# First expert's input from products of tokens with scaled one-hots, gates and clearings taken out of the expert choice's chain, router loads issued from GpSimd

## The chip, the cores and the metric

The kernel runs on one core of a Trainium2 chip. The metric is the device time of one execution in microseconds (us); the number compared is the median of several executions. The chip's engines appear under the profile's names: PE is TensorE (PEld its weight loads), DVE is VectorE, ACT is ScalarE, POOL is GpSimd, SP is SyncE; a "q" behind the name is the engine's own queue of DMA issues and waits.

## What is computed

Two transformer layers over 512 tokens of width 1024. Each layer has a token mixer (the first one sliding-window attention and gated linear attention, the second one block attention), then a mixture of experts: 4 groups of 8 experts, a router that takes one group and the two best experts in it, and a gated hidden layer of 512. The part that matters here, cut from the reference:

```python
def _hier_moe(h, w_group, b_group, w_expert, b_expert, w1, w3, w2):
    g_logits = (xt @ w_group).astype(f32) + b_group.astype(f32)
    g_sel = jnp.argmax(g_logits, axis=-1)
    p_g = jnp.take_along_axis(jax.nn.softmax(g_logits, axis=-1), g_sel[:, None], axis=-1)
    ...
    top_v, top_i = lax.top_k(e_in, MOE_TOPK)
    gate = (p_g * jax.nn.softmax(top_v, axis=-1)).reshape(-1)
    ...
        xr = xt[tok]
        return (jax.nn.silu(xr @ w1[e]) * (xr @ w3[e])) @ w2[e]
# in the layer
h = _rms(x, norm2_w[layer]) * (1 + scale2) + shift2
x = x + gate2 * _hier_moe(h, ...)
```

## The kernel before, in words

The loop over the two layers holds an attention stage and an expert stage. The end of the attention stage makes, for each of four tiles of 128 tokens, the root mean square factor `r2` and the router's logits `lgt` (`norm2`, L587), and writes the scaled tokens to a table in DRAM, `h2d` (L590, from POOL's queue).

The choice (L1000 to L1088) runs mostly on DVE. Three full-size matmuls that nothing reads ("busy", L1002) are put on TensorE at its start. Then come the maxima and one-hots of group and experts, for three tiles together and for the last tile alone, ranks by small matmuls with triangular ones (L1059), and the table `rd` (L1066), which holds for each token and expert its place in that expert's window of 64 slots. Behind `rd`, in the same stretch, the gates are made (L1070 to L1088, with three ACT functions).

The expert stage is in an order written out by hand (`manual_schedule`): each engine takes its instructions as the program states them. It works with pairs of experts, 64 slots each. `select` (L1099) makes a pair's 0/1 matrix from tokens to slots. `gather` (L1132) sums token numbers through it on TensorE and fetches the 128 rows from `h2d` by an indirect DMA on POOL's queue into one of two buffers `xg`; slots without a token get a number out of bounds, and their rows are left as they were, which is why both buffers are cleared before the loop (L1357). `flip_rows` transposes the rows, and `modulate` scales and shifts them into `xT`. For the first pair this stands ahead of the loop: casts of `toknum`, two clearings, two selections and fetches, four more unread matmuls ("py", L1364), then `flip_rows_fast`. In the loop an expert has stage 1 (L1182: 16 products of `xT` with 4 weight tiles), SiLU and product on ACT and DVE, a transpose (L1189), stage 2 (L1202), and the way back into `x_t` (L1219, L1227). For the first expert both slot gates `gs` (L1128) of the first two pairs stand ahead of the product of L1405.

The weights come in 1 MB tiles, six for each expert, through the ring of slots `wA` (3), `wC` (2) and `wB` (13 for each layer, whose memory the attention stage uses before). All are issued on SP's queue (L178 and L181), in order, each when its slot is free: the first four slots of an expert when stage 1 has read them, the other two after stage 2. DMAs issued from SP and from ACT take turns on the same few completion semaphores; one whose turn falls on a semaphore waits until the DMA that had it before has landed. DMAs issued from POOL have others. `load_router` (L114 to L117) loads the router's weights `wr` and biases `br` for a layer, from ACT's queue: for the first layer at the start, for the second one as soon as the first layer's logits (for `br`) and the tables that lie on `wr` (for `wr`) have been used.

## Time and profile before

| | |
|---|---|
| median of 3 runs | 1637.0 us (1635.42 to 1642.87) |
| the profiled execution | 1640.46 us |
| its span, first to last instruction | 1638.7 us |
| mean granted TensorE clock | 0.963 |
| TensorE busy | 1477.0 us, 90% of the span |
| DVE, ACT, POOL busy | 917.0, 514.1, 338.1 us |
| read from HBM | 506.31 MB |

The rows further down are from this one execution; their times are us from the start of its span, its own time is 3.5 us over the median. A stretch's DMA share is the mean busy share of the 16 DMA engines, and PEclk the granted clock of TensorE, where 1.00 is 2.4 GHz and 0.50 is 1.2 GHz. The chain that ended last is followed back by the page only to the branch that closes the second layer's loop; it tells nothing of the stage that is changed, so that stage is read from timelines and stretches.

### The profile page before, as it was taken

What the parts mean: (1) busy time and instruction counts of PE and PEld (TensorE: products, weight loads), DVE (VectorE), ACT (ScalarE), POOL (GpSimd) and SP (SyncE); (2) the same over time, 40 slices, a digit from 0 to 9 for tenths busy, and PEclk for the clock granted to TensorE, in tenths of its full rate; (3) what the DMA queues carried; (4) which work ended last, traced back from release to release, by engine and by line L of the source; (5) the groups of instructions that cost most, each with busy time, mean ns of one, the idle gap of its engine ahead of it and who ended that gap; (6) DMA issues with size and microseconds to landing.
All of it is one profiled execution on the core that took longest, in us unless ns stands there. A gap on an engine that the chain in (4) does not pass through costs nothing. (4 is left out here: it accounts for less than half of the span.)

```text
span 1638.7 us, 20661 instructions
## 1 busy us (share of the span) xinstructions
PE 1477.0 (90%) x7110; PEld 787.5 (48%) x7110; DVE 917.0 (56%) x2034; ACT 514.1 (31%) x1161; POOL 338.1 (21%) x268
## 2 busy tenths in 40 slices
PE   4988888789999999999888988998899999999996
PEld 3665556534444444333366765674344444444333
DVE  3678787636545444444467777554454455545444
ACT  4435532322222222222254344542222222222221
POOL 3433253001111111110043433520011111111110
PEclk9999999889999999999989999998899999999998
DMA  7674364889999999999515634238899999999991
GB/s 280 224 257 157 114 220 157 320 338 417 420 420 420 420 420 420 420 420 421 198 66 181 201 128 147 78 129 339 344 421 419 420 420 419 420 420 420 420 404 59
DMA packets 87674, 504.60 MB, mean 308 GB/s; under 512 B 16434, under 2 KB 18656, under 8 KB 33678
## 3 DMA queue, kind: packets, MB, share of 16 engines
q1 hardware_dynamic: 73900, 486.93, 74.5%
q0 software_dynamic: 6240, 12.77, 2.1%
q10 hardware_dynamic: 7426, 3.54, 0.8%
q8 instruction: 58, 0.95, 0.2%
q14 instruction: 50, 0.41, 0.1%
HBM read 506.31 MB, written 6.32 MB: 313 GB/s over the span
## 5 line engine op out<-in xcount | busy, mean ns | idle before, releaser
L1182 PE MATMUL h<-wB,xT 128*64 128x512 f32 x1584 | 355.9, 594 | 9.3 <-DMA wB<-in_W 8.1
L1182 PEld LDWEIGHTS h<-wB,xT 128*64 128x64 f32 x1584 | 111.2, 137 | 243.3 <-issue 206.4
L1213 POOL TENSOR_TENSOR y<-ytm,y 64x512 fp32r<-64x512 f32 x64 | 81.0, 1265 | 658.2 <-ACT y L1212 658.2
L1202 PE MATMUL py<-wB,gT 128*64 128x512 f32 x736 | 178.9, 631 | 1.2 <-DVE gT L1191 1.0
L1212 ACT CAST y<-ytm 64x512 fp32r<-64x512 f32 x132 | 81.4, 617 | 287.4 <-DVE ytm L1209 285.8
L349 POOL TENSOR_TENSOR wlo<-wA,whi 128x512 fp32r<-128x512 f32 x86 | 122.0, 1423 | 212.9 <-ACT whi L348 104.5
L1227 DVE TENSOR_TENSOR x<-cmb,x 128x512 f32<-128x512 f32 x262 | 162.2, 681 | 2.1 <-PE cmb L1219 2.0
L1219 PE MATMUL cmb<-y,s 128*128 128x512 f32 x512 | 149.3, 415 | 0.0
L1392 ACT ACTIVATE ytm<-h 128x256 f32<-128x256 f32 x66 | 25.3, 384 | 340.6 <-PE h L1182 318.8
L1213 DVE TENSOR_TENSOR y<-ytm,y 64x512 fp32r<-64x512 f32 x68 | 83.1, 1222 | 86.2 <-ACT y L1212 86.2
L368 PE MATMUL pp<-whi,hTh 128*128 128x512 f32 x288 | 119.0, 415 | 5.4 <-ACT raw L405 3.9
L1182 PE MATMUL h<-wA,xT 128*64 128x512 f32 x528 | 118.0, 593 | 1.2 <-DMA wA<-in_W 1.1
L369 PE MATMUL pp<-whi,hTl 128*128 128x512 f32 x288 | 116.8, 409 | 0.4 <-POOL hTl L494 0.4
L1209 DVE SCALAR_TENSOR_TENSOR ytm<-py,gs,g2r 128x512 f32<-128x512 f32 x66 | 49.6, 751 | 119.8 <-PE py L1202 119.8
L318 DVE SCALAR_TENSOR_TENSOR adaacc<-wC,cond,adaacc 128x1024 f32<-128x1024 f32 x70 | 115.2, 1646 | 2.4 <-DMA wC<-in_ada_w 1.0
L1405 DVE TENSOR_TENSOR ytm<-ytm,h 128x256 f32<-128x256 f32 x66 | 27.8, 421 | 136.4 <-ACT ytm L1392 135.4
L1202 PEld LDWEIGHTS py<-wB,gT 128*64 128x64 f32 x736 | 51.3, 144 | 100.7 <-issue 89.6
L1146 ACT ACTIVATE xT<-tr,mc,mc 128x128 f32<-128x128 f32 x256 | 96.2, 457 | 9.2
L370 PE MATMUL pp<-wlo,hTh 128*128 128x512 f32 x288 | 93.5, 412 | 0.5 <-POOL wlo L349 0.4
L1219 PEld LDWEIGHTS cmb<-y,s 128*128 128x128 f32 x512 | 86.8, 189 | 14.7 <-issue 3.2
L348 ACT CAST whi<-wA 128x512 fp32r<-128x512 f32 x88 | 54.3, 619 | 89.5 <-PE pp L369 67.6
L1138 POOL DMA_INDIRECT xg<-h2d,num x34 | 34.4, 1010 | 196.6 <-DVE num L1137 177.0
(382 smaller groups left out, 2133.1 us busy)
## 6 DMA issues: line engine op xcount, KB each, us to landing
wB<-in_W SPq DMA_DIRECT2D x278, 1024.0 KB, 19.8
wA<-in_W SPq DMA_DIRECT2D x66, 1024.0 KB, 19.7
wC<-in_ada_w SPq DMA_DIRECT2D x80, 512.0 KB, 4.9
wC<-in_W SPq DMA_DIRECT2D x40, 1024.0 KB, 19.8
wA<-in_WIN SPq DMA_DIRECT2D x21, 1024.0 KB, 7.6
wA<-in_WOUT SPq DMA_DIRECT2D x8, 1024.0 KB, 4.8
wC<-in_ADAC SPq DMA_DIRECT2D x4, 1024.0 KB, 11.8
h2d<-adaacc POOLq DMA_DIRECT2D x8, 512.0 KB, 4.1
```

The costliest lines, as they stand in the source:

```text
L318: V.scalar_tensor_tensor(acc, w, cond[:, k:k + 1], acc, op0=OP.mult, op1=OP.add))
L349: eng.tensor_tensor(lo, src, hi.bitcast(F32), OP.subtract)
L368: PE.matmul(banks[i], hTh[:, k, ts], hi, start=(k == 0), stop=False),
L369: PE.matmul(banks[i], hTl[:, k, ts], hi, start=False, stop=False)),
L370: lambda i, ts: PE.matmul(banks[i], hTh[:, k, ts], lo, start=False, stop=(k == KT - 1)))
L1146: S.activation(dst, src, AF.Identity, scale=sc2[:, kk:kk + 1], bias=sh2[:, kk:kk + 1])
L1182: PE.matmul(p[64 * h:64 * h + 64, :], xT[:, k, off:off + 64], w[:, k % 2, :, 256 * h:256 * h + 256], start=(k == 0), stop=(k == KT - 1), s ...
L1202: PE.matmul(py[64 * h:64 * h + 64, :], gT[:, kt % 2, 64 * (kt // 2):64 * (kt // 2) + 64], w[:, kt % 2, 512 * h:512 * h + 512], start=(kt = ...
L1212: S.copy(y2[h][hs], yt[hs])
L1213: low[h].tensor_tensor(y2[h][ls], yt[hs], y2[h][hs].bitcast(F32), OP.subtract)
L1219: PE.matmul(p, s2[:, 128 * i:128 * i + 128], y2[h], start=(n == 0), stop=(n == len(parts) - 1))
L1227: V.tensor_tensor(xs, p, xs, OP.add)
```

## The change

- The first pair is no longer fetched for its first expert. `first_rows` makes four one-hots of that expert's 64 slots, each scaled by the tokens' `r2` (4 DVE instructions), and multiplies them with the tokens in `x_t`: 8 blocks of 128 columns by 4 token tiles, 32 matmuls. Each block is modulated from PSUM straight into the first half of `xT`. The transposes of `flip_rows_fast` and the "py" matmuls are gone.
- Between the blocks stand both fetches of the first two pairs (they still serve the second expert and those after), the selections, and the gates, now a generator `gates()` in four steps; tables that they need were moved from a pool that closes to one that stays.
- The clearings of `xg` are gone: a second table `toknum0`, without the offset of 4096, gives slots without a token the number 0, so that token 0's row is fetched for them.
- The second expert's half of `xT` is made by `flip_second` after the first expert's hidden transpose, with the second pair's slot gates and the cast of `toknum`.
- `load_router` issues its four loads from POOL's queue.

```diff
+    toknum0 = cst.tile([P, NT, 2], F32R, name="toknum0")
...
     def load_router(l):
-        S.dma_start(wr[:, :, 0:4], a["moe_w_group"][l].rearrange("(k p) g -> p k g", p=P))
-        S.dma_start(wr[:, :, 4:36], a["moe_w_expert"][l].rearrange("(k p) g -> p k g", p=P))
-        S.dma_start(br[:, 0:4], a["moe_b_group"][l:l + 1, :].broadcast_to([P, 4]))
-        S.dma_start(br[:, 4:36], a["moe_b_expert"][l:l + 1, :].broadcast_to([P, 32]))
+        G.dma_start(wr[:, :, 0:4], a["moe_w_group"][l].rearrange("(k p) g -> p k g", p=P))
+        G.dma_start(wr[:, :, 4:36], a["moe_w_expert"][l].rearrange("(k p) g -> p k g", p=P))
+        G.dma_start(br[:, 0:4], a["moe_b_group"][l:l + 1, :].broadcast_to([P, 4]))
+        G.dma_start(br[:, 4:36], a["moe_b_expert"][l:l + 1, :].broadcast_to([P, 32]))
...
+                    V.tensor_copy(toknum0[:, :, 0:1], tk[:, :, 0:1])
+                    V.tensor_scalar(toknum0[:, :, 1:2], tk[:, :, 1:2], 4096.0, None, op0=OP.add)
...
-            gm, v1, v2, fst = (rtile([NT], n) for n in ("gm", "v1", "v2", "fst"))
+            gm, v1, v2, fst = (mk_.tile([P, NT], F32, name=n) for n in ("gm", "v1", "v2", "fst"))
...
-            ml, mk1, mk2 = (rtile([NT, E], n) for n in ("ml", "mk1", "mk2"))
+            ml = rtile([NT, E], "ml")
+
+            mk1, mk2 = rd2[:, :, 0:E], gd2[:, :, 0:E]
...
+        def gates():
+
+            ge = mk_.tile([P, NT, 4], F32, name="ge")
+            pg, ex, g_1, g_2 = (mk_.tile([P, NT], F32, name=n) for n in ("pg", "ex", "g_1", "g_2"))
+            V.tensor_tensor(ge, gl_, bc(gm, 4), OP.subtract)
             S.activation(ge, ge, AF.Exp)
...
+        def first_rows(xT, sel0, todo):
+
+            sr = mt.tile([P, T], F32R, name="s2", bufs=2).bitcast(F32)[:, 0:NT * WIN]
+            for i in range(NT):
+                V.tensor_scalar(sr[:, WIN * i:WIN * i + WIN], slotrow[:, 0:WIN], rd[:, i, 0:1], r2[:, i:i + 1],
+                                op0=OP.is_equal, op1=OP.mult)
+            sel0()
+            ps_ = [bank("cmb") for _ in range(4)]
+            for k in range(KT):
+                p = ps_[k % 4][:, WIN * (k // 4):WIN * (k // 4) + WIN]
+                for i in range(NT):
+                    PE.matmul(p, x_t[:, i, 128 * k:128 * k + 128], sr[:, WIN * i:WIN * i + WIN], start=(i == 0),
+                              stop=(i == NT - 1))
+                for f in todo.get(k, ()):
+                    f()
+                modulate(xT[:, k, 0:WIN], p, k, (S, V)[k % 2])
...
+        def flip_second(xT, src):
+
+            for q in range(2):
+                ps_ = [bank("cmb") for _ in range(2)]
+                for k in range(4):
+                    PE.transpose(ps_[k % 2][:, 128 * k:128 * k + 128], src[:, 512 * q + 128 * k:512 * q + 128 * k + 128], ident)
+                for k in range(4):
+                    modulate(xT[:, 4 * q + k, 64:128], ps_[k % 2][:, 128 * k + 64:128 * k + 128], 4 * q + k, (V, S)[k % 2])
...
-            for t in rg_two:
-                V.tensor_copy(t[:, :, 0:2], toknum)
-            for t in xg_two:
-                V.memset(t, 0.0)
-            sels = [sel_of(0)]
-            gather(sels[0], 128, rg_two[0][:, :, 0:2], xg_two[0])
-            sels.append(sel_of(1))
-            gather(sels[1], 128, rg_two[1][:, :, 0:2], xg_two[1])
-            pw = bank("py")
-            for _ in range(4):
-                PE.matmul(pw, ones, cf[:, 0:512], start=True, stop=True)
-            for h in range(2):
-                flip_rows_fast(xT, h, xg_two[0])
+            gate_steps = gates()
+            sels = []
+
+            def fetch(n):
+                gather(sels[n], 128, toknum0, xg_two[n], 0.0)
+
+            def step():
+                next(gate_steps, None)
+
+            first_rows(xT, lambda: sels.append(sel_of(0)),
+                       {0: [step], 1: [lambda: fetch(0), lambda: sels.append(sel_of(1))], 2: [step], 3: [step],
+                        4: [lambda: fetch(1), step]})
...
                 if e == 0:
-                    for n in range(2):
-                        p = bank("cmb")
-                        slot_sums(p, sels[n], 128, gates_of(n)[:, :, 2:6])
-                        gs[n] = slot_gates(p)
+                    first_gates(0)
...
+                if e == 0:
+                    flip_second(xTs[0], xg_two[0])
+                    first_gates(1)
```

## Rows read from the trace of the kernel before

**Rows 1.** Busy time of each engine in stretches of the first layer's expert stage and what lies ahead of it: after the times of the engines stand the granted clock, the DMA share and GB/s.
```profile
302.00:312.00 10.00, 7.84 (x48) 5.66 (x47) 6.47 (x30) 4.70 (x8) 1.06 (x2) 1.00 0.30 78
342.00:348.00 6.00, 5.52 (x16) 1.76 (x18) 0.42 (x1) 0.00 (x0) 0.00 (x0) 0.57 0.36 115
362.00:366.00 4.00, 4.00 (x16) 1.31 (x14) 0.19 (x2) 0.00 (x0) 0.00 (x0) 0.72 0.46 142
380.00:785.00 405.00, 390.05 (x1870) 161.73 (x1868) 197.45 (x392) 104.74 (x226) 50.67 (x43) 1.00 1.01 420
```
**Rows 2.** The same for the second layer's expert stage.
```profile
1144.00:1152.00 8.00, 6.52 (x36) 2.87 (x32) 1.26 (x7) 1.89 (x5) 0.00 (x0) 1.00 0.91 351
1152.00:1158.00 6.00, 3.95 (x10) 1.29 (x12) 1.74 (x6) 0.00 (x0) 0.00 (x0) 0.56 0.59 247
1158.00:1172.00 14.00, 10.83 (x51) 3.90 (x48) 8.88 (x32) 3.12 (x7) 2.27 (x2) 0.95 0.89 356
```
**Rows 3.** Who waited for whom from 330 to 800: us in total, times, longest.
```profile
PEld h L1182 <- DMA wB<-in_W: 19.4, 23, 1.4
```
**Rows 4.** SP's queue of weight loads in order of time: start, us, what, count.
```profile
310.76 6.92 SPq L178 DMA_DIRECT2D wB<-in_W  x7
331.64 3.76 SPq L178 DMA_DIRECT2D wA<-in_W  x3
```
**Rows 5.** What SP's queue waited for from 284 to 318: us in total, times, longest.
```profile
SPq L178 <- DMA br<-in_moe_b_group: 21.2, 1, 21.2
```
**Rows 6.** The first layer's choice and the first expert's start, in order of time: start, us, engine, line, what, and the idle time before it with what ended it.
```profile
308.20 2.84 PE L1002 MATMUL busy<-cf,ones 128*128 128x512 f32 x6 [0.35 <-DVE lgt L587]
308.76 0.15 DVE L1012 TENSOR_REDUCE fst<-goh 128x3 f32<-128x12 f32 x1
309.91 0.11 DVE L1013 TENSOR_TENSOR goh<-goh,fst 128x12 f32<-128x12 f32 x1
310.06 0.17 DVE L1048 TENSOR_SCALAR goh<-goh 128x12 f32<-128x12 f32 x1
311.21 0.19 DVE L1049 TENSOR_TENSOR ml<-lgt,goh 128x96 f32<-128x96 f32 x1
312.51 0.23 DVE L1040 TENSOR_SCALAR mk<-mk,fst 128x32 f32<-128x32 f32 x1
315.53 0.29 DVE L1066 TENSOR_TENSOR rd<-prk,md 128x128 f32<-128x128 f32 x1 [0.23 <-PE prk L1059]
319.99 1.09 POOL L1138 DMA_INDIRECT xg<-h2d,num  x1 [8.94 <-DVE sel L1099]
320.73 6.62 PE L1364 MATMUL py<-cf,ones 128*128 128x512 f32 x8
328.61 1.09 PE L1161 MATMUL cmb<-cf,xg 128*128 128x128 f32 x8 [1.26 <-DMA xg<-h2d,num]
329.66 5.37 PE L1182 MATMUL h<-wA,xT 128*64 128x512 f32 x24
342.48 2.83 PE L1202 MATMUL py<-wB,gT 128*64 128x512 f32 x6 [0.52 <-DVE gT L1191]
```
**Rows 7.** The same for the second layer.
```profile
1121.40 4.54 PE L1002 MATMUL busy<-cf,ones 128*128 128x512 f32 x6 [0.35 <-DVE lgt L587]
1128.68 0.29 DVE L1066 TENSOR_TENSOR rd<-prk,md 128x128 f32<-128x128 f32 x1 [0.18 <-PE prk L1059]
1141.89 5.37 PE L1182 MATMUL h<-wA,xT 128*64 128x512 f32 x24
```
**Rows 8.** Stretches with one granted clock (columns as in rows 1: the clock is the last but two).
```profile
311.00:315.00 4.00, 0.05 (x1) 0.00 (x0) 3.97 (x25) 0.00 (x0) 0.05 (x1) 1.00 0.85 238
316.40:326.60 10.20, 7.71 (x15) 4.31 (x16) 2.92 (x14) 1.69 (x3) 2.10 (x2) 0.50 1.02 427
340.30:347.10 6.80, 5.29 (x14) 1.77 (x16) 1.23 (x4) 0.00 (x0) 0.00 (x0) 0.50 0.47 194
1125.40:1128.70 3.30, 1.18 (x16) 0.52 (x14) 3.05 (x20) 0.00 (x0) 0.00 (x0) 1.00 1.02 398
1128.90:1139.00 10.10, 7.04 (x14) 3.97 (x15) 3.56 (x17) 1.91 (x4) 2.08 (x2) 0.50 1.02 426
```
**Rows 9.** Small products with 128x128 weights: the router's logits at the full clock, the weight loads of four sums of token numbers at the lower clock, and the line of these sums with the shortest, median and longest weight load in ns.
```profile
306.80 1.06 PE L586 MATMUL pa<-wr,stg 128*128 128x36 f32 x8
316.72 0.93 PEld L1120 LDWEIGHTS num<-rg,sel 128*128 128x128 f32 x4 [1.23 <-issue]
L1120 PEld LDWEIGHTS num<-rg,sel x136: 186/192/338, 316.7 to 1568.8; 128*128 128x128 f32 x136
```
**Rows 10.** The router's loads on ACT's queue at the second layer's start and what POOL does then, in order of time; POOL's first work after its loads at the kernel's start; and the line of the first of the bias loads, with the shortest, median and longest issue in ns.
```profile
815.96 0.39 ACTq L114 DMA_DIRECT2D wr<-in_moe_w_group  x1
818.53 2.51 POOL L1225 TENSOR_TENSOR x<-x,xg 128x512 f32<-128x512 f32 x2 [22.54 <-ACT xg L1224]
24.00 2.49 POOL L349 TENSOR_TENSOR wlo<-wA,whi 128x512 fp32r<-128x512 f32 x2 [19.31 <-ACT whi L348]
L116 ACTq DMA_DIRECT2D br<-in_moe_b_group x2: 364/2355/4346, 15.8 to 308.2; - x2
```
**Rows 11.** The page's line for POOL's DMA queue (packets, MB, share of 16 engines) and the issues that write the table.
```profile
q0 software_dynamic: 6240, 12.77, 2.1%
h2d<-adaacc POOLq DMA_DIRECT2D x8, 512.0 KB, 4.1
```

More of the change, by code (lines that the diff above doesn't have):

```diff
@@ L506, in tile_hybrid_block @@
                     V.tensor_copy(trib, below)
-                    V.tensor_copy(toknum, cf[:, 544:552].rearrange("p (t c) -> p t c", c=2))
+                    tk = cf[:, 544:552].rearrange("p (t c) -> p t c", c=2)
+                    V.tensor_copy(toknum, tk)
+                    V.tensor_copy(toknum0[:, :, 0:1], tk[:, :, 0:1])
+                    V.tensor_scalar(toknum0[:, :, 1:2], tk[:, :, 1:2], 4096.0, None, op0=OP.add)
             if l == 0:
@@ L994, in rtile @@
                 return rp.tile([P] + shape, dt, name=name)
-            def bc(ap, n):
-                return ap.unsqueeze(2).broadcast_to([P, NT, n])
             pw = ps.tile([P, 512], F32, name="busy", bufs=1)
@@ L1088, in tile_hybrid_block @@
             V.tensor_tensor(gd, mk1[:, :, ::-1], mk2[:, :, ::-1], OP.add)
-        ps = pool(moe, f"mps{l}", bufs=1, space=PSUM)
-        mt = pool(moe, f"mt{l}", side=s2)
-        mu = pool(moe, f"mu{l}", side=s2)
+            yield
+        def first_rows(xT, sel0, todo):
[13 more added lines that the diff above has]
+                modulate(xT[:, k, 0:WIN], p, k, (S, V)[k % 2])
         def select(rdx, m):
@@ L1130, in slot_gates, with gather @@
             return gs
-        def gather(sel, m, rhs, xg):
+        def gather(sel, m, rhs, xg, base=4096.0):
             p = bank("num")
@@ L1136, in gather @@
             num = mu.tile([P, 1], I32, name="num", bufs=2)
-            V.tensor_scalar(num[0:m], p[0:m, 0:1], p[0:m, 1:2], 4096.0, op0=OP.add, op1=OP.add)
+            V.tensor_scalar(num[0:m], p[0:m, 0:1], p[0:m, 1:2], base, op0=OP.add, op1=OP.add)
             G.indirect_dma_start(xg[0:m], None, h2d[l][:], bass.IndirectOffsetOnAxis(ap=num[0:m, 0:1], axis=0),
@@ L1155, in flip_rows @@
                 modulate(xT[:, 4 * q + k, :], p[:, 128 * k:128 * k + 128], 4 * q + k, S)
-        def flip_rows_fast(xT, q, src):
-            ps_ = [bank("cmb") for _ in range(2)]
-            for k in range(4):
-                PE.transpose(ps_[k % 2][:, 128 * k:128 * k + 128], src[:, 512 * q + 128 * k:512 * q + 128 * k + 128], ident)
-            for k in range(4):
-                modulate(xT[:, 4 * q + k, :], ps_[k % 2][:, 128 * k:128 * k + 128], 4 * q + k, (V, S)[k % 2])
+        def flip_second(xT, src):
[5 more added lines that the diff above has]
+                    modulate(xT[:, 4 * q + k, 64:128], ps_[k % 2][:, 128 * k + 64:128 * k + 128], 4 * q + k, (V, S)[k % 2])
         def flip_sel(sel, psn, dst):
@@ L1399, in tile_hybrid_block, with first_gates @@
                     gs[ahead] = slot_gates(gather(sel, 128, rg, xg_two[ahead % 2])[:, 2:6])
+                def first_gates(n):
+                    V.tensor_copy(rg_two[n][:, :, 0:2], toknum)
+                    p = bank("cmb")
+                    slot_sums(p, sels[n], 128, gates_of(n)[:, :, 2:6])
+                    gs[n] = slot_gates(p)
                 if e == 0:
-                    for n in range(2):
-                        p = bank("cmb")
-                        slot_sums(p, sels[n], 128, gates_of(n)[:, :, 2:6])
-                        gs[n] = slot_gates(p)
+                    first_gates(0)
                 V.tensor_tensor(gt, gt, p13[:, 256:512], OP.mult)
```

18 lines of the change are left out of this document (10 added, 8 removed).

## The prediction, made before the changed kernel was built or run

> **What bounds the kernel now.** I read three views, in this order. First the stretches with their DMA share. In both expert stages the DMA engines are full for some 400 us at 420 GB/s (share 1.01) while TensorE waits for weights 23 times [rows 1, 3]: there the end of a stage is the end of its weight stream. What can move that end is time in which the stream stood still. Ahead of the first layer's full stretch I count, as (1 - share) x length: 302 to 312, 7.0 us; 342 to 348, 3.8 us; 362 to 366, 2.2 us; together 13.0 us [rows 1]. In the second layer: 0.7 + 2.5 + 1.5 = 4.7 us between 1144 and 1172 [rows 2]. No gain at the head of a stage can be larger than that.
>
> Second, SP's queue, for why the stream stood still. The first of three refills of wA was issued at 331.64, two us after stage 1 of the first expert began at 329.66, which is when its first slot was read [rows 4, 6]. The gap at 342 to 348 ends when stage 2 of the first expert, begun at 342.48, gives its slots back, and the next one an expert later [rows 1, 6]. So these gaps move with TensorE's first expert: its start is the bound to work on. The gap at 302 to 312 has another cause: SP stood 21.2 us behind the landing of the router's bias load, which waits on ACT's queue for the last logits and holds a completion semaphore whose turn had come; the next seven wB loads left from 310.76 [rows 4, 5].
>
> Third, the timeline from the choice to that start: `rd` ends at 315.82, stage 1 starts at 329.66, 13.8 us later; in the second layer 1128.97 and 1141.89, 12.9 us [rows 6, 7].
>
> **Part 1, clearings and casts out of the choice.** The reduction L1012 ends at 308.91, its successor starts at 309.91; L1048 ends at 310.23, its successor starts at 311.21 [rows 6]. DVE had the two clearings there: 1.0 + 1.0 = 2.0 us; I take 1.9, since a successor doesn't start at once. `rd` then ends at 313.9 and 1127.05. The gates (13 small DVE instructions) go behind the scaled one-hots, beside TensorE's products. The first one-hot takes about 0.25 us (nearest row: 0.23 for 128x32 [rows 6]), so the products start near 314.3 and 1127.4.
>
> **Part 2, products for fetch and transposes.** Removed from the path: the fetch from 319.99 to 328.61 and the transposes up to 329.66 [rows 6]. Added to it: 8 x 4 matmuls, two instructions each, so 64 with a weight load each, and 8 weight loads of the two fetches' sums. The nearest row at the full clock is the router's logits: 8 in 1.06 us, the last one lasting 0.28, so about 0.113 apart [rows 9]. 72 x 0.113 = 8.1 us. At the lower clock the nearest row is four loads in 0.93 us, the last one 0.338: 0.197 apart [rows 9], so 72 x 0.197 = 14.2 us. Which it is decides this change.
>
> The granted clock is 1.00 from 311 to 315, in which TensorE worked 0.05 us, and 0.50 from 316.4 to 326.6. It came back 5.9 us after the unread matmuls of 320.73 began, and at 347.1, 4.6 us after stage 2 began [rows 6, 8]. The change shortens that idle stretch but leaves it: the three "busy" matmuls end at 311.04, the products start at 314.3. So I expect the fall to 1.2 GHz there too, at about the same place, 316.4. Products at a spacing set by weight loads are no full load, and I expect them not to bring the clock back. First layer: 2.1 us at 0.113 are 18 of 72, the other 54 take 10.6 us; stage 1 starts at 327.0 instead of 329.66, but at 1.2 GHz, for the 4.6 to 5.9 us that a recovery took. Half of that is lost, 2.3 to 2.9: an equivalent start at 329.3 to 329.9. **First layer: 0.0 us**, from -0.3 to +0.3.
>
> In the second layer the clock was 1.00 again from 1125.4, since the "busy" matmuls ran until 1125.94, and 0.50 from 1128.9 [rows 7, 8]. Here the gap ahead of the products would be only 1.5 us. Falls at 1128.8: 12 instructions done, 60 x 0.197 = 11.8, start 1140.6, plus 2.6: 1143.2, so +1.3 us. Never falls: start at 1135.5, 6.4 us early, of which the stream can use no more than its 4.7 us [rows 2]. Falls halfway, at 1132: 41 done, 31 x 0.197 = 6.1, start 1138.1, plus 2.6: 1140.7, so -1.2 us. I take the middle one. **Second layer: -1.2 us**, from +1.3 to -4.7.
>
> The skill has a rule against this part: the Trainium skill, "TensorE: Matmul & The Clock Gate", section "Part 1: The HAM clock gate (the "warmup" mystery)", says that throttled is the array's default and that activity releases it; this change takes out work that was there for nothing else. The trace agrees with the rule [rows 8]; by it the first layer's products run slow, which is what the sum above has from rows alone.
>
> **Part 3, what goes beside other work.** Gates, selections and modulations: some 25 DVE instructions, mostly of 0.1 to 0.3 us [rows 6], about 5.5 us by estimate, against at least 8.1 us of products, in the order of the blocks; if DVE came late, stage 1 would start late by the difference. An SiLU table load on ACT stands ahead of the fifth block, which stage 1 reads only halfway through. Both fetches have until the first expert's transposes, over 10 us. The second expert's half (8 transposes, 8 modulations) and the second pair's gates go between the first expert's hidden transpose and stage 2. Before, two gate sums and their DVE work stood ahead of the product there; one goes, 2 us, and eight transposes with modulations come, about as long. I count 0, and -1 to +1 for the range.
>
> **Part 4, fetching token 0 for empty slots.** POOL's queue moved 12.77 MB, of which 8 x 0.52 wrote the table; the rest over 34 fetches is 0.25 MB each, where a full one has 0.52 [rows 11]. Two fetches add up to 0.55 MB for each layer, 1.3 us at 420 GB/s; it falls into stream gaps that stay in this forecast, and only where the gaps close (second layer at the full clock) does it cost.
>
> **Part 5, router loads on POOL.** SP's stop of 21.2 us goes, and the last wB loads start up to 8 us earlier. By itself that buys nothing: the following refill waits for the first expert anyway. It is cover for a gain in part 2. On POOL the `wr` loads stand ahead of its additions to `x_t` at 818.53, from about 815.96 [rows 10]. The issue time for 1024 short runs on POOL is in no row. Between nothing (0.39 on ACT) and the longest issue of a router load, 4.35 on ACT [rows 10], I take under 1.2: two fit into the 2.57 us before 818.53. At the worst both take 8.7 us and delay the second layer by 6.1 us. At the start POOL has nothing until 24.00 and was idle 19.31 us before [rows 10], so four loads cost nothing there.
>
> The Trainium skill, "SBUF — State Buffer", section "Who interferes with whom", states that DVE in a two-port mode locks GpSimd out of the port pair with which it would also write a DMA's descriptors. No row here shows a POOL issue drawn out by it: the fetch issue among DVE's work took 1.09 us [rows 6]. [...]
>
> **Sum.** 0.0 - 1.2 + 0 = -1.2 us. Against the profiled execution's own 1640.46 that is 1639.3; it lies 3.5 over the median 1637.0, so in the frame of the runs 1635.8, rounded 1636.
>
> **The rivals.** (a) The clock holds through the products in both layers. For it: it was granted 1.00 until 316.4, and the gap is shorter. Against: it fell after a gap in every such place of rows 8. First layer: start at 322.4, -7.2, within its 13.0 us; second -4.7, less 1.3 for token 0's rows: -3.4. Together -10.6: 1626. (b) It holds in one layer only: -3.4 or -7.2 with the other layer's falling case: about 1632. (c) Slower: the `wr` loads on POOL hold the additions to `x_t` between the layers. It decides from 1.29 us for each; at 4.35 it costs 6.1: 1642, with the second layer's worse case 1644.5. For: 1024 runs of 16 and of 128 bytes; against: the short loads on ACT there took 0.39. (d) Slower by the clock alone: falls early in both layers and comes back late, +0.3 + 1.3 + 1: 1639.5. (e) The change doesn't do what it says: stage 1 still waits, for modulations or for a bank of PSUM, so the products' gain is nil at any clock: 1637 to 1639.
>
> **How the numbers follow.** Forecast 0.42, (a) 0.12, (b) 0.18, (c) 0.08, (d) 0.12, (e) 0.08. The range 1626 to 1642 holds all but the tails of (a) and (c). A change of 0.5% is 8.2 us, about what a measurement of this kernel can tell from none: faster is (a) and a little of (b), 0.15; slower is the worst of (c), 0.06; the same 0.79.
>
> **What would show it.** The clock granted in the 15 us after `rd`, in each layer: 0.50 there is the forecast, 1.00 is (a). Stage 1's first instruction against `rd`'s end: 13 us by the forecast with a clock still low, 8.5 by (a). The product's spacing, 0.113 or 0.197. No pause in SP's queue before 310. DMA share: the gaps after the first expert's stage 1 stay by the forecast, and shrink by (a). POOL's two issues at the second layer's start, each under 1.29 us. The prediction is wrong if weight loads for products of 64 columns are further apart than these rows, or if products at the lower clock bring the full one back.

## The result and the profile after

The changed kernel took 1649.98 us (median of 4 runs, 1648.4 to 1652.0) against 1636.21 (4 runs, 1635.08 to 1642.87): ratio 1.0077, 95% interval 1.0051 to 1.0102. It is 13.8 us slower, outside the range of 1626 to 1642 and against the direction of the forecast. The profiled execution spans 1649.2 us instead of 1638.7, 10.5 more. In the experiments further down, one run of a_loads_act (5107.85 us) and one of the kernel before beside it (3717.02 us) stand far outside the others, and the ratios leave them out. Landmarks in the two timelines say where they arose (start of the row, for `rd` its end; a landmark's lag is the difference, and a stage's share is what the lag grows by):

| landmark | before | after | lag |
|---|---|---|---|
| first product of the first projection (L368, now L370) | 26.68 | 30.43 | 3.8 |
| last logits but one, first layer (L587, now L592) | 304.67 | 308.98 | 4.3 |
| last logits, first layer | 307.89 | 312.89 | 5.0 |
| `rd` ends | 315.82 | 319.10 | 3.3 |
| first expert, stage 1 / stage 2 | 329.66 / 342.48 | 334.51 / 348.80 | 4.9 / 6.3 |
| last additions of the first layer (L1219, now L1247) | 816.08 | 823.41 | 7.3 |
| last logits, second layer | 1121.09 | 1128.42 | 7.3 |
| `rd` ends | 1128.97 | 1134.63 | 5.7 |
| first expert, stage 1 / stage 2 | 1141.89 / 1154.71 | 1149.79 / 1164.34 | 7.9 / 9.6 |
| last additions of the second layer | 1627.77 | 1638.56 | 10.8 |

So in this pair of profiles 3.8 us are lost in the first 30, a place to which the prediction gave one sentence; 3.5 between there and the end of the first layer, and 3.5 in the second layer's expert stage. The first line is the firm one: in all 14 profiles of this document, the first product comes at 25.9 to 26.7 where the first layer's router loads leave from ACT, and at 30.4 and 30.9 in the two where they leave from POOL. The lags of the next lines, 3 to 8 us, are no larger than what profiles of the same code differ by (last section), so they say less of single stages. The choice itself is 1.7 us shorter in both layers.

First the start. These rows are before (timeline: SP's queue, DVE and TensorE; the loop of seven long sums that makes `adac` is L255, now L257):

```profile
11.44 0.33 SPq L161 DMA_DIRECT2D wA<-in_WIN  x1
15.61 1.93 PE L249 MATMUL pa<-wC,condb 128*32 128x256 f32 x16 [2.07 <-DMA wC<-in_ADAC]
16.03 0.16 DVE L225 SCALAR_TENSOR_TENSOR rt_ln<-ry_ln 128x4 f32<-128x4 f32 x1 [0.74 <-ACT ry_ln L224]
17.60 0.42 DVE L251 COPY adac<-pa 128x256 f32<-128x256 f32 x1 [1.22 <-PE pa L249]
20.17 3.61 DVE L255 SCALAR_TENSOR_TENSOR adac<-wC,cond,adac 128x256 f32<-128x256 f32 x7
26.68 0.80 PE L368 MATMUL pp<-whi,hTh 128*128 128x512 f32 x1
```

And these are the same steps after, with POOL's row and the first of the loads that moved:

```profile
4.66 0.97 POOL L116 DMA_DIRECT2D wr<-in_moe_w_group  x1
5.93 0.47 SPq L163 DMA_DIRECT2D wA<-in_WIN  x1
16.39 1.93 PE L251 MATMUL pa<-wC,condb 128*32 128x256 f32 x16 [1.99 <-DMA wC<-in_ADAC]
18.38 0.42 DVE L253 COPY adac<-pa 128x256 f32<-128x256 f32 x1 [2.89 <-PE pa L251]
18.72 0.15 DVE L227 SCALAR_TENSOR_TENSOR rt_ln<-ry_ln 128x4 f32<-128x4 f32 x1
22.17 5.37 DVE L257 SCALAR_TENSOR_TENSOR adac<-wC,cond,adac 128x256 f32<-128x256 f32 x7
23.33 2.89 POOL L351 TENSOR_TENSOR wlo<-wA,whi 128x512 fp32r<-128x512 f32 x2 [12.85 <-ACT whi L350]
30.43 0.79 PE L370 MATMUL pp<-whi,hTh 128*128 128x512 f32 x1
```

The reader is to see three things. The router's loads leave at 4.66 instead of 12.91. SP's own loads shift with them: the first 1 MB of `wA` leaves at 5.93 instead of 11.44, while `wC` is still on its way. The first product on `wC` starts 0.8 us later; whether the router's loads or the earlier `wA` hold `wC` back, no run separates. On DVE the planner (what sets the order of each engine's instructions before the run) has put the token norm's `rt_ln` behind the copy that waits for that product (18.72 after the copy; before it ran at 16.03, ahead of it). Together the seven long sums on `wC` start 2.0 us later, and now they meet POOL's first additions: they last 5.37 instead of 3.61, 1.76 more. 2.0 + 1.76 is the 3.75 us at the first product, to a hundredth. The Trainium skill, "SBUF — State Buffer", section "Who interferes with whom", has the rule for this last part: a DVE instruction with two SBUF inputs contends with a GpSimd instruction that reads SBUF, and the later one waits. The trace agrees: the two of the seven sums that fall beside POOL's additions take 1.37 us, the others 0.485, and the additions 1.48 and 1.45 instead of 1.26.

The first layer's choice and first expert after (timeline); [rows 6] answer to them:

```profile
308.98 0.25 DVE L592 SCALAR_TENSOR_TENSOR lgt<-pa,r,br 128x36 f32<-128x36 f32 x1 [1.47 <-PE pa L591]
310.01 1.15 ACT L594 ACTIVATE adaacc<-x,r 128x1024 f32<-128x1024 f32 x1 [1.32 <-DMA h2d<-adaacc]
318.81 0.29 DVE L1070 TENSOR_TENSOR rd<-prk,md 128x128 f32<-128x128 f32 x1 [0.23 <-PE prk L1063]
319.60 3.03 PE L1116 MATMUL cmb<-s,x 128*128 128x64 f32 x16 [0.73 <-DVE s L1109]
320.81 1.15 ACT L594 ACTIVATE adaacc<-x,r 128x1024 f32<-128x1024 f32 x1 [8.98 <-DVE ge L1085]
322.25 0.54 POOL L595 DMA_DIRECT2D h2d<-adaacc  x1 [7.71 <-ACT ex L1088]
323.24 5.36 PE L1116 MATMUL cmb<-s,x 128*128 128x64 f32 x24
329.22 5.36 PE L1116 MATMUL cmb<-s,x 128*128 128x64 f32 x24
330.09 1.08 POOL L1165 DMA_INDIRECT xg<-h2d,num  x1 [7.30 <-DVE gd L1101]
334.51 6.76 PE L1210 MATMUL h<-wA,xT 128*64 128x512 f32 x24
```

The second layer's, answering to [rows 7]:

```profile
1134.34 0.29 DVE L1070 TENSOR_TENSOR rd<-prk,md 128x128 f32<-128x128 f32 x1 [0.18 <-PE prk L1063]
1135.13 2.79 PE L1116 MATMUL cmb<-s,x 128*128 128x64 f32 x16 [0.75 <-DVE s L1109]
1138.53 5.36 PE L1116 MATMUL cmb<-s,x 128*128 128x64 f32 x24
1149.79 7.01 PE L1210 MATMUL h<-wA,xT 128*64 128x512 f32 x24
1164.34 4.53 PE L1230 MATMUL py<-wB,gT 128*64 128x512 f32 x10
```

And stretches after (columns as in [rows 1], the clock is the last but two), answering to [rows 8] and to the first and last of [rows 1]:

```profile
302.00:312.00 10.00, 8.64 (x58) 7.37 (x58) 5.09 (x14) 4.57 (x10) 1.08 (x2) 1.00 0.87 346
316.80:320.00 3.20, 1.84 (x20) 1.02 (x19) 2.83 (x15) 0.00 (x0) 0.00 (x0) 0.99 1.03 425
320.40:337.10 16.70, 16.70 (x73) 14.76 (x74) 4.73 (x24) 4.34 (x9) 2.65 (x3) 0.50 0.75 280
1136.20:1153.00 16.80, 16.80 (x73) 14.48 (x74) 4.40 (x24) 3.30 (x8) 2.09 (x2) 0.50 1.00 417
400.00:780.00 380.00, 366.87 (x1762) 152.76 (x1759) 182.02 (x354) 98.59 (x213) 47.18 (x40) 1.00 1.01 419
```

Three things are to be seen here. The products begin at the full clock, and about 1 us later it is 0.50 (within 0.8 us in the first layer, 1.1 in the second), through all the rest of them and at least the first 2.6 and 3.2 us of stage 1, although TensorE is busy for every microsecond of that time. The 72 instructions of products and sums take 14.9 and 14.7 us. Stage 1's first 24 instructions take 6.76 and 7.01 us where they took 5.37. The second thing is in ACT's rows: the scaled tokens of the last two tiles wait for the landing of earlier writes of the table. (The row at 320.81 names DVE, which ended at the same moment; its semaphore is that of the write issued at 311.45, whose packets end at 320.1, 8.7 us later. Before, the write issued at 305.72 had its last packet at 308.3.) The stream stands still no longer at 302 to 312 (DMA share 0.87 instead of 0.30), so these writes share the DMA engines with it: the page gives 7.0 us to landing where it gave 4.1 [rows 11], and the first layer's last write leaves 9.4 us after the last logits instead of 2.6, the fetch 17.2 us after them instead of 12.1. The third is the last row: 419 GB/s in the full stream where [rows 1] have 420.

### The profile page after: what moved, and what is told of

Read it like the earlier page. It is cut to its first block, busy times and chain, and to the rows that moved or that the text cites. A ratio compares the mean times of both kernels' runs of the same rounds, so it can differ in the third digit from the quotient of the medians.

```text
span 1649.2 us, 20905 instructions
## 1 busy us (share of the span) xinstructions
PE 1496.2 (91%) x7222; PEld 811.2 (49%) x7222; DVE 920.8 (56%) x2048; ACT 516.4 (31%) x1169; POOL 344.5 (21%) x276
## 3 DMA queue, kind: packets, MB, share of 16 engines
q0 software_dynamic: 6528, 14.16, 2.4%
## 5 line engine op out<-in xcount | busy, mean ns | idle before, releaser
L1247 PE MATMUL cmb<-y,s 128*128 128x512 f32 x512 | 149.2, 415 | 0.0
L370 PE MATMUL pp<-whi,hTh 128*128 128x512 f32 x288 | 118.9, 415 | 5.5 <-ACT raw L407 3.9
L1247 PEld LDWEIGHTS cmb<-y,s 128*128 128x128 f32 x512 | 86.8, 189 | 14.7 <-issue 3.2
L1210 PEld LDWEIGHTS h<-wA,xT 128*64 128x64 f32 x528 | 38.1, 140 | 79.3 <-issue 72.6
```

The source lines that it names most:

```text
L370: PE.matmul(banks[i], hTh[:, k, ts], hi, start=(k == 0), stop=False),
L1210: PE.matmul(p[64 * h:64 * h + 64, :], xT[:, k, off:off + 64], w[:, k % 2, :, 256 * h:256 * h + 256], start=(k == 0), stop=(k == KT - 1), s ...
L1247: PE.matmul(p, s2[:, 128 * i:128 * i + 128], y2[h], start=(n == 0), stop=(n == len(parts) - 1))
```

## The experiments

In the order of the table, four kernels at a time were run beside the kernel before on one chip (its medians there: 1636.09, 1637.12, 1636.81; beside the changed kernel 1636.21). The ratio is to it, with its 95% interval, and need not be the quotient of the two medians; kernels of different groups are compared by their ratios.

| kernel | median, us | ratio |
|---|---|---|
| changed | 1649.98 | 1.0077 [1.0051, 1.0102] |
| a_loads_act: changed, loads on ACT | 1641.92 | 1.0028 [1.0016, 1.0039] |
| b_loads_pool: before, loads on POOL | 1645.69 | 1.0052 [1.0038, 1.0066] |
| a_fetch_kept: a_loads_act without the products | 1640.08 | 1.0021 [1.0008, 1.0035] |
| a_dense_rows: a_loads_act, products turned round | 1634.4 | 0.9986 [0.9971, 1.0] |
| a_start_act: changed, first layer's loads on ACT | 1642.62 | 1.0036 [1.0019, 1.0053] |
| a_more_busy: a_loads_act, five unread matmuls | 1637.09 | 1.0002 [0.9986, 1.0017] |
| b_two_br: before, two bias tiles | 1641.02 | 1.0028 [1.0011, 1.0046] |
| a_dense_early: a_dense_rows, transposes behind stage 2 | 1633.69 | 0.9965 [0.9944, 0.9987] |
| b_shift32: before, all tiles 32 bytes further | 1637.32 | 1.0003 [0.9987, 1.0019] |
| a_cleared: a_loads_act, buffers cleared on POOL | 1649.31 | 1.007 [1.0053, 1.0087] |
| a_dense_best | 1629.06 | 0.9958 [0.9942, 0.9974] |
| a_dense_best_pool | 1630.66 | 0.9963 [0.995, 0.9976] |

From one profile of each, in us after the start of the last logits' row (first layer, then second):

| kernel | stage 1 | stage 2 | last additions |
|---|---|---|---|
| before | 21.8, 20.8 | 34.6, 33.6 | 508.2, 506.7 |
| changed | 21.6, 21.4 | 35.9, 35.9 | 510.5, 510.1 |
| a_loads_act | 22.5, 21.4 | 37.3, 35.9 | 508.9, 510.8 |
| a_more_busy | 20.4, 20.0 | 34.5, 34.3 | 508.9, 508.4 |
| a_fetch_kept | 21.5, 20.4 | 36.2, 34.4 | 507.6, 508.4 |
| a_dense_rows | 14.2, 13.9 | 32.0, 31.5 | 506.5, 504.4 |
| a_dense_early | 13.7, 17.9 | 25.7, 30.6 | 504.0, 507.8 |
| a_dense_best | 14.4, 13.4 | 24.5, 23.6 | 502.7, 500.9 |
| b_two_br | 20.3, 21.4 | 33.1, 34.2 | 505.8, 505.8 |

**Loads back on ACT.**

```diff
     def load_router(l):
-        G.dma_start(wr[:, :, 0:4], ...
+        S.dma_start(wr[:, :, 0:4], ...
```

> The changed kernel with the router's four loads back on ACT's queue, everything else as changed. Theory A (the move of the loads itself shifts the kernel's start: in the changed kernel the first logits come 4.0 us later than before, 220.0 against 216.0, and the last logits of the first layer another 1.0 us later, because the weight stream now runs while the table is written): the start is back at 216, the wait of 21.2 us in SP's queue is back, and the time is 1650.0 - 5 = about 1645. Rival B (the start moved because of the two extra casts for the second table of token numbers, and the loads are harmless): the start stays at 220, the time stays at 1649 to 1650.

Measured 1641.92, less than A gave: by the ratios (1.0077 and 1.0028) 8.0 us of 12.6 go, and 4.6 over the kernel before stay. The first product is back at 26.52 with both casts for the second table still in it, so A holds for the start and rival B falls.

**Loads alone on POOL.** The opposite edit to the kernel before.

> The kernel before with only the router's four loads moved to POOL's queue. Theory A: the first logits at 220 instead of 216, the table's writes land later since the weight stream no longer stands still at 302 to 312, about 1641. Rival B (the loads alone change nothing): 1636 to 1637. Rival C (the prediction's own view: the stream's earlier refills are worth a little): 1634 to 1636.

1645.69, 1.0052: 8.5 us by the ratio, more than A gave it. The two halves of the change add up: 1.0028 + 1.0052 against 1.0077. The start shows the same two marks as the changed kernel, the late sums and their length (timeline):

```profile
22.61 5.37 DVE L255 SCALAR_TENSOR_TENSOR adac<-wC,cond,adac 128x256 f32<-128x256 f32 x7
30.88 0.80 PE L368 MATMUL pp<-whi,hTh 128*128 128x512 f32 x1
325.54 0.54 POOL L590 DMA_DIRECT2D h2d<-adaacc  x1 [7.21 <-ACT ge L1071]
334.17 1.09 POOL L1138 DMA_INDIRECT xg<-h2d,num  x1 [8.08 <-DMA h2d<-adaacc]
```

Its fetch waits for the last write of the table, which the kernel before's did not.

**The fetch kept.** Clearings and gates stay out of the choice, token 0's rows are fetched, the products go.

```diff
-            first_rows(xT, ...)
+            sels.append(sel_of(0)); step(); fetch(0)
+            sels.append(sel_of(1)); fetch(1)
+            ... # other gate steps, four unread matmuls
+            for h in range(2):
+                flip_rows_fast(xT, h, xg_two[0])
```

> The changed kernel without the products and with the loads on ACT: the first expert's rows come by the fetch and the transposes again, with the four unread matmuls; clearings, casts and gates stay out of the choice, empty slots fetch token 0. Theory A (the choice is 1.7 us shorter, and the fetch no longer waits for the gates' instructions on DVE, together 3 us earlier for the first expert of each layer; token 0's rows give back 1.3 us of stream for each layer): about 1633. Rival B (the fetch then waits for the landing of the last table write, issued 9.5 us before it in the kernel before, and the stream's gaps close only in part): 1636 to 1639. Rival C (token 0's rows cost more than the bytes): over 1640.

1640.08, 1.0021: between B and C, and slower than the kernel before; A falls. The fetch leaves 10.4 us after the last logits instead of 12.1 and 11.9, yet stage 1 comes only 0.3 and 0.4 earlier, from the fetch's issue to stage 1 it takes 11.1 and 10.0 us for 9.7 and 8.9 (all rows of the pair are fetched now; that this is the reason was only argued). Stage 2 comes 1.6 and 0.8 later. Against a_loads_act (1.0028) the intervals overlap: the products in place of the fetch are worth nothing that these runs can tell, in either direction.

**Products turned round.** One-hots as weights, tokens streamed.

```diff
-            for k in range(KT):
-                for i in range(NT):
-                    PE.matmul(p, x_t[:, i, 128 * k:128 * k + 128], sr[:, WIN * i:WIN * i + WIN], ...)
+            for i in range(NT):
+                for h in range(2):
+                    PE.matmul(p[64 * h:64 * h + 64, :], sr[:, WIN * i:WIN * i + WIN],
+                              x_t[:, i, 512 * h:512 * h + 512], ...)
+            ... # copy to SBUF, four transposes, eight modulations
```

> The changed kernel with the loads on ACT and the products turned round: the one-hots are the weights (64 columns) and the tokens are streamed, 512 columns at a time, two halves side by side, 8 products instead of 32; then one copy to SBUF, four transposes and eight modulations. Theory A (the products are long because they are many small weight loads at the lower clock, 14.9 us; the same multiplications by 16 instructions of 512 columns, as in stage 1, take 3.5 us at 0.22 and 7 at half the clock, and the copy, transposes and modulations 2.4): stage 1 starts about 5.5 us earlier than in the changed kernel, and with full-sized products the clock is back during stage 1: 1635 to 1638. Rival B (what delays the first expert is not the products but the modulations or the rest of its chain): 1644 to 1646, as with the loads alone back on ACT.

1634.4, 7.5 under a_loads_act and a little under A's range; A holds. Timeline of its first layer:

```profile
312.55 3.65 PE L1115 MATMUL cmb<-x,s 128*64 128x512 f32 x16 [0.95 <-DVE s L1109]
319.78 7.01 PE L1222 MATMUL h<-wA,xT 128*64 128x512 f32 x24
330.85 0.66 PE L1192 MATMUL tr<-cf,xg 128*128 128x128 f32 x4 [2.35 <-DMA xg<-h2d,num]
```

The same multiplications take 3.65 us at the full clock, and stage 1 starts 14.2 and 13.9 us after the last logits instead of 21.6 and 21.4. Stage 2 gains less: TensorE then waits 2.35 us for the second fetch.

**Only the first layer's loads back on ACT.**

```diff
-        G.dma_start(...)
+        (S, G)[l].dma_start(...)
```

> The changed kernel with only the first layer's router loads (those at the start) back on ACT's queue; the second layer's stay on POOL's. Theory A (both moves cost: the one at the start 4.0 us, where it puts DVE's first long sums beside POOL's additions; the one in the first layer the rest, since without SP's stop the table's writes land in 9 us instead of 3): 1650.0 - 4.0 = 1646. Rival B (all of the 8 us that the loads' move cost is paid at the start): 1642, like the kernel with all loads on ACT. Rival C (the start is not what the time hangs on): 1650.

1642.62, 1.0036: B. Of the 0.49% that the loads cost in the changed kernel (1.0077 against 1.0028) 0.41 come back with the first layer's loads alone, those at the start (its first product is at 26.31). The second layer's loads are left with 0.08%, within the two intervals.

**Five unread matmuls in the choice.**

```diff
-            for _ in range(3):
+            for _ in range(5):
                 tc.keep_in_program_order(PE.matmul(pw, ones, cf[:, 0:512], ...))
```

> The changed kernel with the loads on ACT and five unread full-size matmuls at the start of the choice in place of three, so that TensorE is busy nearly up to the ranks. Theory A (the products are long because they run at the lower clock, and it falls because TensorE idles in the choice): with the clock kept, the 72 instructions take 8 to 9 us instead of 14.7, stage 1 starts some 6 us earlier and runs at the full clock: 1633 to 1636 against 1641.9. Rival B (products of 64 columns let the clock fall whatever ran before them): it falls within the products, and the time stays at 1640 to 1642.

1637.09, 1.0002, by the ratios 4.3 under a_loads_act: between the two. Timeline and stretches of the first layer:

```profile
316.73 1.97 PE L1116 MATMUL cmb<-s,x 128*128 128x64 f32 x16 [0.95 <-DVE s L1109]
318.96 5.36 PE L1116 MATMUL cmb<-s,x 128*128 128x64 f32 x24
324.93 5.36 PE L1116 MATMUL cmb<-s,x 128*128 128x64 f32 x24
```

```profile
312.00:318.90 6.90, 5.35 (x41) 3.59 (x39) 5.42 (x29) 0.74 (x4) 0.53 (x1) 1.00 0.81 264
319.10:332.50 13.40, 13.40 (x58) 11.78 (x60) 4.18 (x21) 2.70 (x5) 2.11 (x2) 0.50 1.01 419
```

At the full clock the first 16 take 1.97 us, the 0.113 apart of the prediction; 2.3 us after they began the clock falls, and the other 48 are 0.21 apart. So A's price holds and B's mechanism too: an idle choice brings the fall forward, but these products let the clock fall by themselves, with TensorE 100% busy (13.40 of 13.40 us). That it is the products is borne out by a_dense_best below: behind the same five unread matmuls its wide products keep the full clock in both layers.

**Two bias tiles, before.** This takes away SP's wait of [rows 5] without moving a load.

```diff
-    br = cst.tile([P, 36], F32, name="br")
+    brs = [cst.tile([P, 36], F32, name=f"br{n}") for n in range(2)]
```

> The kernel before with a tile of its own for each layer's router biases, so that the second layer's bias load needs nothing of the first layer's last logits: SP's wait of 21.2 us goes, by that alone, with all loads left on ACT. Theory A (the stream that no longer stands still at 302 to 312 makes the table's writes land in 9 us instead of 3; they hold ACT's buffer, and the fetch waits for the last of them): the first expert starts 2 to 4 us later, about 1638. Rival B (the prediction's: nothing changes, since the next refill waits for the first expert anyway): 1636. Rival C (the 7 us of stream are a gain by themselves): 1630 to 1633.

1641.02, 1.0028, slower than A gave it, and not seen to be for A's reason: from the last logits to the last additions it needs 505.8 and 505.8 us instead of 508.2 and 506.7; as the first layer's last logits come 1.3 us later after those before them, about 1 us is left in each layer as a gain. The first expert starts 1.4 us earlier after the last logits in the first layer, without SP's stop. A loss shows at the start: from 40 to 80 us its matmuls run 4.9 us behind those of the kernel before, from 80 to 290 some 3.2 (medians of the pairs). The second layer's bias loads now leave at 23.39 and 23.84, so this too is an edit of the order at the start; the seven sums on `wT` begin at 32.20 instead of 31.46 and last 5.59 instead of 4.54, with two of them stretched beside POOL's additions instead of one. But this profile as a whole is 1.0 us shorter than the one of the kernel before (1637.7, 1638.7), so that the start makes the 4.6 us of the ratio is not shown.

**Transposes behind stage 2.** To a_dense_rows; that the sums of token numbers move too is not in the cut.

```diff
-                if pr + 1 < NP: ... flip_rows(xTs[pr + 1], odd, ...)
+                if pr + 1 < NP: ... if e > 0: flip_rows(xTs[pr + 1], odd, ...)
...
-                if e == 0: flip_second(xTs[0], xg_two[0]); first_gates(1)
...
+                stage2(..., mid=flip_second for e == 0)
+                if e == 0: flip_rows(xTs[1], 0, xg_two[1]); first_gates(1)
```

> The kernel with the turned products (tokens streamed, loads on ACT), with one order changed: the first pair's number sums stand between the products, the second's right behind them, and the transposes of the fetched rows (second expert's half, and the next pair's) go behind stage 2 of the first expert, where before TensorE waited 2.35 us for the second fetch ahead of the first expert's hidden transpose. Theory A (in the kernel with turned products stage 1 started 7.5 us earlier than in the changed kernel after the last logits, but stage 2 only 3.9: the rest stood behind the fetch, the second half and its gates): stage 2 comes about 24 us after the last logits instead of 32, and the second layer's stream gaps close: 1629 to 1632 against 1634.4. Rival B (the stream can't use an earlier stage 2, the gaps only move): 1634.

1633.69, B's figure; by the ratio, 0.9965 against 0.9986 for a_dense_rows, between A and B, with intervals that overlap. Stage 2 comes 25.7 us after the last logits in the first layer, as A says. In the second layer of this profile the clock was 0.50 from 1127 to 1144, and with it the products took twice as long (each half 3.68 us, 1.94 in the first layer) and stage 2 came at 30.6. One half and a stretch from there:

```profile
1132.68 3.68 PE L1117 MATMUL cmb<-x,s 128*64 128x512 f32 x8
1130.30:1133.70 3.40, 3.40 (x12) 1.34 (x10) 0.91 (x4) 0.00 (x0) 0.00 (x0) 0.50 1.02 429
```

So wide products, too, ran at the lower clock from their first to their last, 1128.1 to 1136.4, when it was low at their start.

**All tiles 32 bytes further, before.**

```diff
     toknum = cst.tile([P, NT, 2], F32R, name="toknum")
+    spare32 = cst.tile([P, 8], F32, name="spare32")
+    G.memset(spare32, 0.0)
```

> The kernel before with an idle tile of 32 bytes in each partition put where the change puts its second table of token numbers, so that everything allocated behind it, the weight slots too, lies 32 bytes further, as in the changed kernel. In all traces with that table an 8 KB packet of the weight queue takes 315.4 ns on average in the full stream, without it 314.4, which is 418.6 against 420.0 GB/s. Theory A (it is the place of the slots): packets of 315.4 ns here too, 1.3 us longer in each layer's full stream, 1638 to 1639. Rival B (it is something else in the changed code, the rows of token 0 for instance): packets of 314.4 ns, 1636 to 1637.

A for the rate: packets of 315.3 ns, and this row where the kernel before has 420:

```profile
400.00:780.00 380.00, 366.25 (x1758) 152.65 (x1756) 183.41 (x358) 98.17 (x213) 45.91 (x39) 1.00 1.01 419
```

B for the time, which stays at 1.0003 [0.9987, 1.0019]: 0.3% of two full streams of some 400 us is 2.4 us, inside that interval. 32 bytes more ahead of everything allocated behind them, the weight slots among it, are enough for the slower stream, and nothing else of the change is needed; what it costs was not resolved.

**Buffers cleared on POOL, no rows of token 0.**

```diff
+            for t in xg_two:
+                G.memset(t, 0.0)
...
-                gather(sels[n], 128, toknum0, xg_two[n], 0.0)
+                gather(sels[n], 128, toknum, xg_two[n])
```

> The changed kernel with the loads on ACT, and the first two fetches as before the change: empty slots get a number out of bounds, and the two buffers are cleared, now on POOL and ahead of the choice's end, so that the choice stays short. Theory A (token 0's rows cost 0.5 MB of stream in each layer, 1.3 us, and make the fetch longer): 1639 to 1640 against 1641.9 of the kernel with the loads on ACT. Rival B (the rows fall into gaps of the stream and cost nothing): 1641.5 to 1642.5.

1649.31, by the ratios 6.9 over a_loads_act: neither; the edit brought a cost of its own. Timeline of the second layer's choice, DVE and POOL:

```profile
1129.01 2.19 DVE L1038 TENSOR_SCALAR goh<-goh,fst 128x4 f32<-128x4 f32 x1
1129.15 2.06 DVE L1015 TENSOR_TENSOR goh<-goh,fst 128x12 f32<-128x12 f32 x1
1129.32 1.86 POOL L1384 MEMSET xg<- 128x1024 f32 x2
```

DVE's step of 0.2 to 0.3 us takes 2 us beside POOL's clearings, so `rd` ends 1.9 us later after the last logits than in the changed kernel, and in the first layer 0.7: the stop that the change took out of DVE comes back from POOL. These 2.6 us are not the whole cost; the rest is not located. What token 0's rows cost stays open; their 0.5 MB for each layer are in POOL's queue (14.16 MB, of them 0.3 router loads, against 12.77).

**All of the good parts together.** a_dense_early with five unread matmuls and the table of token numbers padded to 160 bytes; then the same with the second layer's loads on POOL.

```diff
-    toknum0 = cst.tile([P, NT, 2], F32R, name="toknum0")
+    toknum0 = cst.tile([P, 20, 2], F32R, name="toknum0")[:, 0:NT, :]
```

> Turned products, transposes behind stage 2, loads on ACT, five unread matmuls in the choice, and the second table of token numbers padded to 160 bytes, so that the weight slots lie where they lie in the kernel with two bias tiles, whose packets took 314.3 ns. Theory A: 420 GB/s, so 2.6 us less than in the kernel with the transposes behind stage 2 (1633.7), and the clock kept through the choice and the products in both layers, which that kernel's second layer lost from 1126.9 on: about 1629. Rival B (neither the place nor the unread matmuls matter): 1633 to 1634.

> The same with the second layer's router loads on POOL's queue (the first layer's stay on ACT's). Theory A (SP's wait of 21 us ahead of the first layer's choice goes, and the first expert, which needs no fetch, starts early enough to use the stream that comes earlier): 3 to 4 us less than the same kernel with all loads on ACT, about 1626. Rival B (the table's writes, which then land in 9 us, hold the fetch and with it the second expert by as much): no difference. Rival C (POOL's issues between the layers hold the additions to the tokens): slower by 1 to 2.

1629.06, 0.9958 [0.9942, 0.9974]: 7.8 us faster than the kernel before by the medians, 6.9 by the ratio; A. Its timeline and two stretches:

```profile
314.17 1.94 PE L1117 MATMUL cmb<-x,s 128*64 128x512 f32 x8 [0.73 <-DVE s L1109]
320.94 5.37 PE L1220 MATMUL h<-wA,xT 128*64 128x512 f32 x24 [0.33 <-DVE xT L1185]
```

```profile
400.00:780.00 380.00, 366.18 (x1757) 151.72 (x1754) 182.27 (x354) 97.89 (x211) 47.18 (x40) 1.00 1.01 420
1114.00:1146.00 32.00, 23.96 (x118) 10.18 (x118) 16.66 (x80) 7.97 (x21) 3.87 (x4) 1.00 1.01 413
```

The clock is 1.00 from the second layer's choice through stage 2, and the stream stands still for none of it (1.01); the rate is 420 again. With the second layer's loads on POOL it is 1630.66, 0.9963: no difference, as rival B says; the reason that it gives is not shown.

## Why the prediction was wrong

**The step that failed** is in part 5: "At the start POOL has nothing until 24.00 and was idle 19.31 us before, so four loads cost nothing there." POOL had time; but loads are also transfers and places in an order. With them on POOL's queue SP's first weights leave in other places of time and the first product on `wC` starts 0.8 us later, the planner puts DVE's work in another order, and DVE's sums run into POOL's additions. Shown by runs: the loads' move alone costs 8.5 us (b_loads_pool), and 0.41 of the 0.49%, 6.7 of 8 us, come back with those of the first layer (a_start_act). Read from traces only: that it is the late sums and their meeting with POOL, 3.75 us, in both kernels with these loads on POOL and in none of the other twelve. From the first product to the first logits no cost of the move shows: 264.1 us against 263.6 before with the clock at 0.50 for 23.9 us of each, and 266.7 (b_loads_pool) against 267.1 (a_loads_act) with 30.7. The rest of the 7 to 8 us is not located: intervals of a_start_act and of the changed kernel are wide enough for 4.

The other 4.6 us (a_loads_act) stand against a forecast of -1.2. They are not the products' alone, since 3.4 stay with the fetch in their place (a_fetch_kept); how they divide between token 0's rows, the weight slots' place and the clock stays open. The clock's part can be estimated: in the 82 runs of the kernel before that stand beside the experiments, 0.001 more of mean granted clock goes with 0.85 us less, by a straight line through the runs. a_loads_act has a mean of 0.9643 against 0.9680, which would be 3.1 us; b_loads_pool has 0.9660, which would be 1.7, so most of the loads' cost is not the clock's.

**Part 1** was right: 1.7 us for 1.9.

**Part 2** had the mechanism and mis-sized one term. The products did run at 1.2 GHz, with 0.21 between them for 0.197. But the first layer's "18 of 72" at the full clock were only a few, and in the second the case that fell early came, whose +1.3 the prediction had beside its middle case of -1.2; stage 2 came 2.3 us later there. The recovery came about 3 us into stage 1 and not 4.6 to 5.9. Against a kept fetch (a_fetch_kept) the products are a draw. The forecast's premise, "Products at a spacing set by weight loads are no full load", is borne out by a_more_busy, where the clock fell within them. Rival (a), a clock that holds through the products, came only in kernels with other, wide products (a_dense_rows, a_dense_best).

**Part 3** holds: stage 2 followed stage 1 by 14.3 and 14.6 us instead of 12.8, and 1.4 and 1.6 of this is stage 1 at the lower clock. **Part 4** had the bytes right; their cost was not separated.

**Part 5's other steps.** SP's wait did go; "by itself that buys nothing" is near: b_two_br gains about 1 us in each layer and is slower as a whole, and a_dense_best_pool gains nothing. What was missed is that the stream then runs beside the table's writes, so in the changed kernel the last one leaves 6.7 us later after the last logits, and the fetch 5.1. The first expert didn't need them any more; in b_loads_pool it did, and its stage 2 came 3.2 us later. Rival (c) didn't come: POOL's two issues at the layers' boundary, among DVE's additions, took 0.95 and 0.92 us (0.97 and 0.94 at the start), and the lag over it stayed at 7.3.

Not foreseen: a table of 32 bytes that moves the weight slots and lowers the stream's rate by 0.3%.

## What to carry to other kernels

A load that is moved to an idle queue is not free because the queue is idle: ask which other loads change their time with it, which instructions the planner reorders, and which engine's work then meets another's. Look at the first 30 us as closely as at the stage that the change is about. Where a product of many small matmuls runs at the lower clock, turn it round so that the wide operand is streamed before looking for ways to warm the clock. At the lower clock 16 instructions of 512 columns took 7.4 us (a_dense_early) where 64 of 64 columns took 13.2 (14.9 less two sums of 0.86); at the full one they took 3.65, where 64 small ones would take 7.2 at the 0.113 apart of a_more_busy. Shape and clock are worth about a factor of two each here.

## What was not expected of the hardware

TensorE at 100% busy for 16.7 us stayed at 1.2 GHz when most of its instructions were matmuls of 64 columns, each with a weight load; in a_more_busy it fell to it 2.3 us after such products had begun at the full clock.

Code that two kernels share differs by up to 8 us between profiles, by where the lower clock falls: the first logits come at 288.0 in a_dense_rows and at 296.0 in a_dense_early. From the first product to these logits the shortest of the 14 profiles takes 262.1 us, with the clock at 0.50 for 13.7 us of it, the kernel before 263.6 with 23.9, and the longest 269.6 with 37.5. The same part of the first attention stage in the profiles of a_start_act and a_dense_early:

```profile
228.00:250.00 22.00, 19.69 (x122) 13.24 (x122) 16.95 (x40) 3.41 (x11) 9.54 (x7) 0.92 0.49 155
```

```profile
228.00:250.00 22.00, 19.71 (x100) 13.30 (x98) 12.42 (x35) 2.47 (x8) 6.40 (x6) 0.69 0.34 109
```

In the same 22 us the second did 100 matmuls for the first one's 122; the first logits come 5 us later in it. The Trainium skill, "TensorE: Matmul & The Clock Gate", section "Part 1: The HAM clock gate (the "warmup" mystery)", says that the watch over activity runs free of the kernel, so that the same kernel shows different numbers of slow matmuls; these two rows agree. One profile can't tell a gain of 4 us here; medians of a dozen runs can.

The place of a weight slot in SBUF goes with the rate of its load: an 8 KB packet of the full stream took 314.4 ns (before), 314.2 with 160 bytes more ahead of the slots (a_dense_best) and 315.3 with 32 (b_shift32).
